# W_out's split weights in slices of h, its row splits one half ahead, and the modulation products spread over the convolutions

## The chip, the cores and the metric

The kernel runs on one core of one Trainium2 chip. The core has TensorE (PE, matrix products; PEld is its weight load), VectorE (DVE), ScalarE (ACT), GpSimd (POOL) and SyncE (SP, here a queue that issues DMAs). The engines run independently, each through its own queue in order, and wait for each other by semaphores. The metric is the device time of one execution in microseconds (us).

## The reference

One layer of an encoder over 1024 rows of 1024 features, all in float32:

```python
mod = c_act @ w_ada + b_ada
sh_m, sc_m, g_m, sh_f, sc_f, g_f = split(mod, 6)
h = rmsnorm(x, norm_mix_w) * (1 + sc_m) + sh_m
z, xbc, dt_raw, q, k, v = split(h @ w_in)
y_ssd = ssd_mixer(z, xbc, dt_raw, ...)      # causal conv width 4, silu, state-space scan, gate, norm
y_att = chunk_attention(q, k, v, rel_bias)  # 8 heads of 64, own chunk and 8 before
x = x + g_m * (concat[y_ssd, y_att] @ w_out)
h = rmsnorm(x, norm_ffn_w) * (1 + sc_f) + sh_f
x = x + g_f * conv_ffn(h, w_up, ffn_conv_w, w_down)
return rmsnorm(x, final_norm_w)
```

## The kernel before

Every large product is made of three TensorE products (`mm3`, lines 56 to 58): each float32 operand is split into a rounded high part and a low rest (`split`, lines 65 and 66: ACT writes the high part, DVE or POOL the rest), and high x high, high x low and low x high are added up. A tile is 128 rows by up to 512 columns. The order of the instructions on each engine is made by a planner, which simulates the program with its own costs and issues what is ready by them; `tc.issue_after(i)` adds the rule that something comes behind instruction i on i's engine.

The stages in order:

1. The norm of x, h = `hth`, `htl` (eight feature blocks by 1024 rows, high and low), and q, k, v of head pairs 0 and 1.
2. `attention(p)` for four pairs of heads, in steps u = 0 to 3 of two row tiles. Pairs 2 and 3 get their q, k, v by products put between the steps of pairs 1 and 2. `attention(3)` has none; there the modulation products are issued.
3. A modulation product is `mod_col`: a load of one 128 x 1024 block of w_ada on SP, and one DVE instruction (line 114) that multiplies it by the activated c and sums along the rows. Of 48 column blocks, 16 are made in stage 1. `MODS` says how many are made in each step of `attention(3)`, from four buffers of the tag qk. The last eight (`G_F`) come in four of the convolutions, two each, from the buffers `wos`.
4. Eight calls of `conv_silu` (B, C and the SSD inputs): a product of h with a block of W_in into one of two PSUM tiles `s`, then ACT (L421), three DVE sums (L423), tanh on ACT (L428) and two DVE products (L429). Each has its weights loaded by `wu_pair` (L129) and split by ACT and POOL.
5. z = h @ W_z in two column halves, `z_tile(1, st)` and `z_tile(0, st)`, st the row tile. Each reads column slice st of `hth` and `htl`. Beside the second half come `row_of` (turns eight columns of the gate into a row broadcast over partitions), `dt_prep` (softplus of dt, decays), the first chunk's `ssd_pre`, and the first W_out weights.
6. The SSD scan, chunk by chunk (`ssd_chunk`), and the output product, row tile by row tile (`wout_tile`), which the planner lays between each other. W_out is cut into eight pieces (dh, j): column half dh, and two of the eight feature blocks. Each piece is loaded, multiplied by the gate row on DVE (L518, the fold) and split (L65, L66). y_a's rows (part 0) and the SSD's (part 1, in `xs`) are split beside the products (`yh`, `yl`). After the tile follow the sum with x (L748) and `norm_row`.
7. The feed-forward part: w_up with the gated convolution, w_down, the final norm.

Before, two W_out pieces (column half 0, y_a) are split into the buffers `wh`, `wl` of the convolution weights; the other six go to tiles `woh`, `wol` of the pool `wop`, which takes the space of `hth` and `htl` and opens when z is done. The staged raw pieces lie in `wos` (three) and `raws` (two).

## Time and profile before

| | |
|---|---|
| median of 3 runs | 1259.03 us (1258.4 to 1260.23) |
| the profiled execution | 1259.93 us, span 1258.2 us |
| mean granted TensorE clock | 0.982 |
| PE busy | 1181.4 us (94%), 5786 products |
| PEld busy | 988.0 us (79%) |
| DVE busy | 954.1 us (76%) |
| ACT busy | 560.3 us (45%) |
| POOL busy | 196.6 us (16%) |
| DMA | 150.86 MB, mean 120 GB/s |

The profile is of one execution. Its slices are 40 equal parts of the span, with the busy share in tenths. A stage table gives the busy time of each engine between two times, then the granted TensorE clock (1.00 is full speed), the share of time that the DMA engines were busy, and GB/s. A row of the waits names who waited for whom, the total, how often, and the longest. Products on TensorE overlap at their ends, so that the duration of one (389 ns) is longer than the step from one to the next.

### The profile page before, as it was taken

The page shows a single profiled execution, that of the slowest core. Times are in us where ns is not written, and L with a number is a line of the kernel's source. Part 1 is how long each engine was busy: PE and PEld are TensorE (multiplying, and loading weights), DVE is VectorE, ACT ScalarE, POOL GpSimd, SP SyncE. Part 2 cuts the span into 40 slices and gives each one's busy share as a digit, 9 for nine tenths or more (in the row PEclk, how much of TensorE's full clock was granted, in tenths as well). Part 3 has the DMA queues.
Part 4 walks back from the last instruction along what each step waited for, and adds up shares of the span by engine and source line. Part 5 has one row for each costly group of instructions (what it writes and reads, how often), then busy time and mean ns, then how long its engine had stood idle before and what let it go on. Part 6 is the DMA issues. An engine that isn't in the chain of part 4 may idle for free.

```text
span 1258.2 us, 15608 instructions
## 1 busy us (share of the span) xinstructions
PE 1181.4 (94%) x5786; PEld 988.0 (79%) x5786; DVE 954.1 (76%) x1452; ACT 560.3 (45%) x917; POOL 196.6 (16%) x174
## 2 busy tenths in 40 slices
PE   5898999979999979999799999999999999999995
PEld 3686788857889968888578888888888888888884
DVE  7836554599576886764999898888898879766976
ACT  4526554653333453434644444533344435433443
POOL 1304563764120032210000000000000000000002
PEclk9999999999999989999999999999999999999998
DMA  9712121336232212221213322223323286834433
GB/s 341 257 25 66 56 61 45 128 124 228 84 99 104 102 34 67 68 67 67 92 42 126 126 95 93 90 101 126 126 78 107 84 300 225 301 107 137 163 122 133
DMA packets 57835, 150.86 MB, mean 120 GB/s; under 512 B 5792, under 2 KB 5920, under 8 KB 56352
## 3 DMA queue, kind: packets, MB, share of 16 engines
q1 hardware_dynamic: 50704, 125.49, 29.3%
q10 hardware_dynamic: 7056, 24.38, 4.8%
q8 instruction: 45, 0.74, 0.2%
q14 instruction: 30, 0.25, 0.1%
HBM read 116.56 MB, written 29.10 MB: 116 GB/s over the span
## 4 chain that ended last, share of the span: by engine, by line
PE 80%; DVE 11%; ACT 3%; issue 2%; DMA 2%; POOL 0%; SPq 0%; DVEq 0%; POOLq 0%; ACTq 0%
PE dn L57 6%; PE dn L56 6%; PE dn L58 5%; PE uY L56 5%; PE uY L58 5%; PE uY L57 5%; PE uZ L58 3%; PE uZ L57 3%; PE uZ L56 3%; PE uX L58 3%; PE uX L57 3%; PE uX L56 3%; PE acc L56 3%; PE acc L57 3%; PE acc L58 3%; PE wops L56 2%
## 5 line engine op out<-in xcount | busy, mean ns | idle before, releaser
L765 POOL TENSOR_TENSOR st<-st,mhalf 128x1 f32<-128x1 f32 x16 | 12.4, 777 | 679.5 <-DVE st L764 679.5
L56 PE MATMUL dn<-w 128*128 128x512 f32 x308 | 111.9, 389 | 0.0
L57 PE MATMUL dn<-w 128*128 128x512 f32 x308 | 111.9, 389 | 0.0
L325 POOL TENSOR_SCALAR p<-p,st 128x640 f32<-128x640 f32 (+4 forms) x64 | 103.0, 1623 | 31.5 <-DVE st L324 26.2
L58 PE MATMUL dn<-w 128*128 128x512 f32 x308 | 103.3, 389 | 0.0
L65 ACT ACTIVATE w<-ya 128x1024 fp32r<-128x1024 f32 (+1 forms) x44 | 41.8, 950 | 98.4 <-PE uY L58 89.5
L56 PEld LDWEIGHTS dn<-w 128*128 128x128 f32 x308 | 57.8, 188 | 12.0
L58 PEld LDWEIGHTS dn<-w 128*128 128x128 f32 x308 | 57.8, 188 | 12.0
L57 PEld LDWEIGHTS dn<-w 128*128 128x128 f32 x308 | 57.8, 188 | 11.9
L65 ACT ACTIVATE w<-xs 128x1024 fp32r<-128x1024 f32 (+1 forms) x44 | 41.8, 951 | 40.5 <-PE uY L58 30.1
L319 DVE CUSTOM_DVE_ANT_0 p<-s,bias 128x640 f32<-128x640 f32 (+4 forms) x64 | 40.6, 650 | 23.5 <-PE tp L351 8.7
L65 ACT ACTIVATE pt<-tp 128x512 fp32r<-128x512 f32 (+2 forms) x72 | 36.4, 522 | 48.4 <-PE tp L351 23.3
L66 DVE TENSOR_TENSOR pt<-tp,pt 128x512 fp32r<-128x512 f32 (+2 forms) x72 | 41.9, 596 | 20.4 <-ACT pt L65 13.3
L322 ACT ACTIVATE p<-p,st 128x640 f32<-128x640 f32 (+4 forms) x64 | 44.1, 690 | 21.1 <-DVE st L319 20.2
L66 DVE TENSOR_TENSOR w<-ya,w 128x1024 fp32r<-128x1024 f32 (+1 forms) x44 | 47.8, 1087 | 5.1 <-ACT w L65 5.1
L56 PE MATMUL s<-hth,wh 128*128 128x512 f32 x128 | 51.6, 403 | 0.2 <-DVE bt L423 0.2
L907 DVE SCALAR_TENSOR_TENSOR a<-cv,pkt,a 128x1023 f32<-128x1023 f32 (+1 forms) x40 | 51.1, 1277 | 0.1
L57 PE MATMUL s<-htl,wh 128*128 128x512 f32 x128 | 51.0, 398 | 0.0
L58 PE MATMUL s<-hth,wl 128*128 128x512 f32 x128 | 50.8, 396 | 0.0
L907 DVE SCALAR_TENSOR_TENSOR a<-cg,pkt,a 128x1023 f32<-128x1023 f32 (+1 forms) x40 | 49.5, 1278 | 0.0
L66 POOL TENSOR_TENSOR wl<-raws,wh 128x1024 fp32r<-128x1024 f32 x14 | 33.9, 2422 | 89.0 <-ACT wh L65 89.0
L66 DVE TENSOR_TENSOR w<-xs,w 128x1024 fp32r<-128x1024 f32 (+1 forms) x44 | 47.7, 1085 | 0.0
(410 smaller groups left out, 3592.1 us busy)
## 6 DMA issues: line engine op xcount, KB each, us to landing
qk<-in_w_ada_dram SPq DMA_DIRECT2D x24, 512.0 KB, 4.7
gz<-a ACTq DMA_DIRECT2D x10, 1024.0 KB, 5.3
adat<-in_w_ada_dram SPq DMA_DIRECT2D x16, 512.0 KB, 5.7
ya<-in_w_up_dram SPq DMA_DIRECT2D x10, 768.0 KB, 4.0
xs<-in_w_up_dram SPq DMA_DIRECT2D x10, 768.0 KB, 4.0
raws<-in_w_ft_dram SPq DMA_DIRECT2D x14, 512.0 KB, 3.5
gy<-a ACTq DMA_DIRECT2D x10, 512.0 KB, 2.6
qk<-in_x_dram SPq DMA_DIRECT2D x8, 512.0 KB, 6.3
```

The costliest lines, as they stand in the source:

```text
L56: T.matmul(ps, lh, rh, start=start, stop=False, skip_group_check=more)
L57: T.matmul(ps, lh, rl, start=False, stop=False, skip_group_check=more)
L58: T.matmul(ps, ll, rh, start=False, stop=stop, skip_group_check=more)
L65: i = A.activation(hi, src, AF.Copy) if ehi is A else ehi.tensor_copy(hi, src)
L66: return i, elo.tensor_tensor(lo, src, f32(hi), ALU.subtract)
L319: V.tensor_tensor_reduce(out=dst, in0=src, in1=bsl, scale=-1.0, scalar=3e38, op0=ALU.add, op1=ALU.min, accum_out=nm)
L322: A.activation(pv_, pv_, AF.Exp, scale=-1.0, bias=nm, accum_out=rs)
L325: G.tensor_scalar(pv_, pv_, rr, None, op0=ALU.mult)
L765: G.tensor_tensor(r, ms, mhalf[:, 0:1], ALU.pow)
L907: V.scalar_tensor_tensor(a[:, j:S], c[:, 0:S - j], w[2 - j], a[:, j:S], op0=ALU.mult, op1=ALU.add)
```

## The change

- Modulation: `MODS` goes from (0, 4, 4, 16) to (0, 2, 2, 10), with the gate of the mixer first; the other 18 products, G_F's eight among them, are made after each of the eight convolutions (`CMODS`, 2 or 3 each) from the three `wos` buffers. `affn` and `bffn` are computed after the z stage.
- W_out: every piece is split into a slice of `hth` and `htl` of 128 columns (slot j of the order `WORDER`), over all eight feature blocks. Slot j is read by z row tile j, so it is free once that tile is done in both halves. Raw pieces lie in a ring of three `wos` and two `raws` buffers. The gate row and the first three loads and folds move to the first z half; the splits of these three come behind `dt_prep`'s own split (`pin`), the other five folds and splits behind the last ACT and DVE instructions of the first `ssd_pre`. `dt_prep` moves from z row tile 2 to 0 of the second half, `ssd_pre` from 4 to 3, the second gate row from 1 to 3. The pool of h is closed only after the feed-forward sums.
- `wout_tile`: the split rows of y lie in one tile (two buffers, in the convolution weights' space), and are made one half-tile ahead of their products; x comes as one 128 x 1024 load in place of two of 128 x 512.

```diff
@@ -23,10 +23,10 @@
 FFN = 2816
 NF = FFN // P
 EPS = 1e-6
-WZB, ROWST, ROWST2, DTST, WOST = 4, 0, 1, 2, 3
+WZB = 4
 PB = (2, 2, 1, 3)
-FOLD = (1, 1, 1, 1)
-MODS = (0, 4, 4, 16)
+MODS = (0, 2, 2, 10)
+CMODS = (2, 2, 2, 2, 2, 2, 3, 3)
 PRST = 4
 GP, GPL = {0: (0,1), 2: (2,)}, ()
 XL = (3, 4, 5, 6)
@@ -370,7 +370,7 @@
                         tl.rearrange("p (a b) -> p a b", a=2), ALU.add)
 
     last_v, early = [], {}
-    mtq, todo = [], [(m + kt) for kt in range(KT) for m in (G_M, SC_F, SH_F)]
+    mtq, todo = [], [m + kt for m in (G_M, SC_F, SH_F, G_F) for kt in range(KT)]
 
     def attention(p, extra=()):
         extra = dict(extra)
@@ -468,11 +468,20 @@
     na = bcp.tile([P, 16], F32, name="na")[:, 0:8]
     wos = bcp.tile([P, 3, D], F32, name="wos")
     es_t = ExitStack()
+    wosc, stc_, pin = [0], [0], []
+
+    def stage():
+        i, stc_[0] = stc_[0] % 5, stc_[0] + 1
+        return wos[:, i, :] if i < 3 else raws[:, i - 3, :]
+
+    def conv_mods(n, at):
+        for _ in range(CMODS[n]):
+            wosc[0] += 1
+            mod_col(todo.pop(0), wos[:, wosc[0] % 3, :], at)
+
     for g in range(2):
-        conv_silu(4 + g, bt_[g], th512)
-        conv_silu(6 + g, ct_[g], th512)
-    mod_scale(affn, SC_F, NFFN, 0, KT)
-    mod_shift(bffn, SH_F, 0, KT)
+        conv_mods(2 * g, conv_silu(4 + g, bt_[g], th512))
+        conv_mods(2 * g + 1, conv_silu(6 + g, ct_[g], th512))
     sgt_ = th512()[:, 0:P]
     G.memset(ones, 1.0)
     G.affine_select(out=tle, in_=ones, compare_op=ALU.is_ge, fill=0.0, base=0,
@@ -483,9 +492,7 @@
     sgt = f32(sgtr)
     for ft in range(4):
         xt = bcp.tile([P, S], F32, tag="rm", bufs=2, name="xst")
-        at = conv_silu(ft, xt, th512)
-        for i in range(2):
-            mod_col(G_F + 2 * ft + i, wos[:, i, :], at)
+        conv_mods(4 + ft, conv_silu(ft, xt, th512))
         for hh in range(2):
             tps = tp_tile()
             for j in range(4):
@@ -493,33 +500,25 @@
                             ident)
             A.activation(xs[:, 4 * hh:4 * hh + 4, ft * P:(ft + 1) * P],
                          tps.rearrange("p (a b) -> p a b", a=4), AF.Copy)
-    wop_ = []
-    wosc = [0]
     halves = [slice(0, 512), slice(512, 1024)]
     order = [4, 5, 6, 7, 0, 1, 2, 3]
-
-    def wout_weights(dh, js):
-        ws = []
-        for j in js:
-            if dh == 0 and j < 2:
-                wh = wu.tile([P, 1024], F32R, tag="wh", name="wh")
-                wl = wu.tile([P, 1024], F32R, tag="wl", name="wl")
-            else:
-                wh = wop_[0].tile([P, 1024], F32R, tag=f"woh{dh}{j}", name="woh")
-                wl = wop_[0].tile([P, 1024], F32R, tag=f"wol{dh}{j}", name="wol")
-            if (dh, j // 2) != (0, 0) and wosc[0] < 3:
-                t = wos[:, wosc[0], :]
-                wosc[0] += 1
-            else:
-                t = raw_tile()
-            for b in range(2):
-                nc.sync.dma_start(t[:, b * 512:(b + 1) * 512], w_out[order[2 * j + b], :, halves[dh]])
-            tv = t.rearrange("p (a b) -> p a b", a=2)
-            (V if FOLD[j] else G).tensor_tensor(
-                tv, tv, rowb[:, halves[dh]].unsqueeze(1).to_broadcast([P, 2, 512]), ALU.mult)
-            split(wh, wl, t, A, V)
-            ws += [(wh[:, 0:512], wl[:, 0:512]), (wh[:, 512:1024], wl[:, 512:1024])]
-        return ws
+    ws = [[], []]
+
+    def wout_load(dh, j):
+        t = stage()
+        for b in range(2):
+            nc.sync.dma_start(t[:, b * 512:(b + 1) * 512], w_out[order[2 * j + b], :, halves[dh]])
+        return t
+
+    def wout_fold(dh, t):
+        tv = t.rearrange("p (a b) -> p a b", a=2)
+        V.tensor_tensor(tv, tv, rowb[:, halves[dh]].unsqueeze(1).to_broadcast([P, 2, 512]), ALU.mult)
+
+    def wout_split(dh, t, slot):
+        c = slice(slot * P, slot * P + P)
+        with tc.issue_after(pin[0]), tc.issue_after(pin[1]):
+            split(hth[:, :, c], htl[:, :, c], t.rearrange("p (a b) -> p a b", b=P), A, V)
+        ws[dh] += [(hth[:, k:k + 4, c], htl[:, k:k + 4, c]) for k in (0, 4)]
 
     def rm512():
         return bcp.tile([P, S], F32, tag="rm", bufs=2, name="gt")[:, 0:512]
@@ -575,7 +574,7 @@
         V.scalar_tensor_tensor(sm["adt"].rearrange("p (c h) -> p c h", c=8),
                                sm["dt"].rearrange("p (c h) -> p c h", c=8), -1.0,
                                na.unsqueeze(1).to_broadcast([P, 8, 8]), op0=ALU.mult, op1=ALU.mult)
-        split(adh, adl, sm["adt"], A, V)
+        pin[:] = [i.ins for i in split(adh, adl, sm["adt"], A, V)]
         dps = tp_tile()
         for i, m in enumerate((tle, sgt, ones)):
             T.matmul(dps[:, 64 * i:64 * i + 64], m, sm["adt"], start=True, stop=True)
@@ -614,39 +613,47 @@
             for i in range(2):
                 T.matmul(sg, sgtr, rm[:, i].rearrange("p h l -> p (h l)"), start=i == 0, stop=i == 1)
             m = th512().rearrange("p (h l) -> p h l", h=4)
-            A.activation(m, sg.rearrange("p (h l) -> p h l", h=4), AF.Exp)
-            V.tensor_tensor(m, m, cb[:, g:g + 1, :].to_broadcast([P, 4, P]), ALU.mult)
+            pin1 = A.activation(m, sg.rearrange("p (h l) -> p h l", h=4), AF.Exp)
+            pin2 = V.tensor_tensor(m, m, cb[:, g:g + 1, :].to_broadcast([P, 4, P]), ALU.mult)
             ms_.append(m)
+        pin[:] = [pin1.ins, pin2.ins]
         return xdt, xdd, cb, ms_
 
     wz = wz_weights(1)
+    gcol = const.tile([P, 16], F32, name="gcol")
+    gbias = [pkt[:, B_ADA + o:B_ADA + o + 8] for o in (G_M, G_F)]
+    V.tensor_tensor(gcol[:, 0:8], modc[:, G_M:G_M + 8], gbias[0], ALU.add)
+    WORDER = [(0, 0), (0, 1), (1, 0), (1, 1), (0, 2), (0, 3), (1, 2), (1, 3)]
+    wt = []
     for st in range(NT):
         z_tile(1, st, wz)
+        if st == 0:
+            row_of(gcol[:, 0:8], rowb, ps1, "tp", 2, ones, rm512)
+            wt += [wout_load(*w) for w in WORDER[0:3]]
+        if st in (3, 4, 5):
+            wout_fold(WORDER[st - 3][0], wt[st - 3])
     wz = wz_weights(0)
-    gcol = const.tile([P, 16], F32, name="gcol")
-    gbias = [pkt[:, B_ADA + o:B_ADA + o + 8] for o in (G_M, G_F)]
-    V.tensor_tensor(gcol[:, 0:8], modc[:, G_M:G_M + 8], pkt[:, B_ADA + G_M:B_ADA + G_M + 8], ALU.add)
     for st in range(NT):
         z_tile(0, st, wz)
-        if st == ROWST:
-            row_of(gcol[:, 0:8], rowb, ps1, "tp", 2, ones, rm512)
-        if st == DTST:
+        if st == 0:
             dt_prep()
-        if st == ROWST2:
+        if st == 3:
+            for j in range(3):
+                wout_split(WORDER[j][0], wt[j], j)
+            pre0 = ssd_pre(0, tp_tile, tp_tile)
             V.tensor_tensor(gcol[:, 8:16], modc[:, G_F:G_F + 8], gbias[1], ALU.add)
             row_of(gcol[:, 8:16], rowa, ps1, "tp", 2, ones, rm512)
-        if st == PRST:
-            pre0 = ssd_pre(0, tp_tile, tp_tile)
-        if st == WOST:
-            ws0 = wout_weights(0, (0, 1))
+    for j in range(3, NT):
+        wt.append(wout_load(*WORDER[j]))
+        with tc.issue_after(pin[1]):
+            wout_fold(WORDER[j][0], wt[j])
+        wout_split(WORDER[j][0], wt[j], j)
     es_t.close()
     es_p1.close()
-    es_ht.close()
 
 
     es_w = ExitStack()
     wop = es_w.enter_context(tc.tile_pool(name="wop", bufs=1, side="left", reuse_waits="tile"))
-    wop_.append(wop)
     es_p2b = ExitStack()
     ps2b = es_p2b.enter_context(tc.tile_pool(name="ps2b", bufs=1, space=PSUM, side="left",
                                              reuse_waits="tile"))
@@ -726,35 +733,38 @@
             for j, g in enumerate(names):
                 gd[g, m] = t[:, :, j, :]
 
-    ws = [ws0, []]
-    ws[1] += wout_weights(1, (0, 1))
-    ws[0] += wout_weights(0, (2, 3))
-    ws[1] += wout_weights(1, (2, 3))
+    mod_scale(affn, SC_F, NFFN, 0, KT)
+    mod_shift(bffn, SH_F, 0, KT)
+    xr_, yq, dg = {}, {}, {}
+
+    def wout_rhs(st, part):
+        if st < NT:
+            y = yq[st, part] = wu.tile([P, 2, 4, P], F32R, tag="wh", name="yhl")
+            split(y[:, 0], y[:, 1], x1[part][:, st, :].rearrange("p (a b) -> p a b", a=4), A, V)
+
     def wout_tile(st):
-        xr = [wop.tile([P, 512], F32, tag="xr", bufs=2, name="xr") for _ in range(2)]
-        for dh in range(2):
-            nc.sync.dma_start(xr[dh], x[st * P:(st + 1) * P, halves[dh]])
+        xr = xr_[st] = wu.tile([P, 2, 512], F32, tag="wl", name="xr")
+        nc.sync.dma_start(xr.rearrange("p a b -> p (a b)"), x[st * P:(st + 1) * P, :])
         ps = [ps2b.tile([P, 512], F32, tag="wo", bufs=PB[0], name="wops") for _ in range(2)]
+        if st == 0:
+            wout_rhs(0, 0)
         for part in range(2):
-            yh = wop.tile([P, 4, P], F32R, tag="yh", bufs=3, name="yh")
-            yl = wop.tile([P, 4, P], F32R, tag="yl", bufs=3, name="yl")
-            split(yh, yl, x1[part][:, st, :].rearrange("p (a b) -> p a b", a=4), A, V)
+            y = yq.pop((st, part))
+            wout_rhs(st + part, 1 - part)
             for dh in range(2):
                 for k in range(4):
                     w = ws[dh][4 * part + k]
-                    mm3(ps[dh], yh[:, k, :], yl[:, k, :], w[0], w[1], part == 0 and k == 0,
-                        part == 1 and k == 3)
+                    mm3(ps[dh].rearrange("p (a b) -> p a b", a=4), y[:, 0, k, :], y[:, 1, k, :],
+                        w[0], w[1], part == 0 and k == 0, part == 1 and k == 3)
         for dh in range(2):
-            V.tensor_tensor(x1[dh][:, st, :], ps[dh], xr[dh], ALU.add)
+            V.tensor_tensor(x1[dh][:, st, :], ps[dh], xr[:, dh, :], ALU.add)
             nc.scalar.dma_start(x1d[st * P:(st + 1) * P, halves[dh]], x1[dh][:, st, :])
 
-    dg = {}
-
     def norm_row(st):
-        junk = wop.tile([P, 512], F32, tag="xr", bufs=2, name="junk")
+        junk = xr_.pop(st)
         m = [stat(), stat()]
         for dh in range(2):
-            A.activation(junk, x1[dh][:, st, :], AF.Square, scale=1.0 / 32.0, accum_out=m[dh])
+            A.activation(junk[:, dh, :], x1[dh][:, st, :], AF.Square, scale=1.0 / 32.0, accum_out=m[dh])
         r = rstd2(m)
         dg[st] = wop.tile([P, P], F32, tag="dg", bufs=8, name="dg")
         V.tensor_scalar(dg[st], ident, r, None, op0=ALU.mult)
@@ -964,6 +974,7 @@
     h_raw((7,))
     sums(slice(384, 512))
     es_w.close()
+    es_ht.close()
     es_l.close()
     fp = ctx.enter_context(tc.tile_pool(name="fp", bufs=1, side="left", reuse_waits="tile"))
     c_tile("v")
```

## The prediction

> **What bounds the kernel now.** I read the 40 slices (31.5 us each) first, then busy time by stage, then TensorE's waits and the queues around the worst of them.
>
> ```profile
> PE   5898999979999979999799999999999999999995
> DVE  7836554599576886764999898888898879766976
> 262.00:284.00 22.00, 13.59 (x79) 12.24 (x78) 21.48 (x54) 11.60 (x27) 17.19 (x8) 0.87 0.54 189
> 284.00:316.00 32.00, 29.74 (x155) 25.07 (x155) 30.14 (x51) 10.94 (x20) 14.84 (x6) 0.98 0.64 216
> 316.00:391.00 75.00, 75.00 (x360) 62.87 (x360) 46.11 (x59) 26.71 (x42) 10.72 (x7) 0.98 0.31 106
> 391.00:414.00 23.00, 23.00 (x192) 22.76 (x191) 13.24 (x27) 6.83 (x15) 0.00 (x0) 1.00 0.14 48
> 414.00:442.30 28.30, 28.30 (x218) 26.44 (x217) 24.81 (x48) 14.51 (x37) 2.05 (x2) 1.00 0.32 112
> 442.30:463.50 21.20, 14.75 (x62) 10.81 (x60) 16.82 (x19) 13.28 (x28) 9.24 (x7) 0.76 0.15 51
> 463.50:570.00 106.50, 103.75 (x531) 87.61 (x532) 72.85 (x115) 37.49 (x97) 25.30 (x33) 1.00 0.18 60
> 600.00:640.00 40.00, 30.97 (x139) 24.23 (x138) 39.56 (x55) 22.62 (x32) 0.00 (x0) 0.96 0.18 64
> ```
>
> The stage rows give length, then busy time of PE, PEld, DVE, ACT, POOL, then granted clock and DMA. PE is the bound nearly everywhere. It dips to 7 tenths in three slices after the start (numbers 9, 15 and 20). The first (the last head pair's attention, 262 to 316) and the third (600 to 640) are stages in which DVE has no free time. In the second, where z ends and W_out begins (442.3 to 463.5), PE stands still for 21.20 - 14.75 = 6.45 us. The change touches the first two and leaves the third. What stands still costs twice, by the clock:
>
> ```profile
> 266.00:268.00 2.00, 0.73 (x6) 0.49 (x4) 2.00 (x5) 1.37 (x3) 2.00 (x1) 1.00 0.12 25
> 268.00:270.00 2.00, 0.00 (x0) 0.00 (x0) 2.00 (x3) 0.00 (x0) 1.18 (x1) 1.00 0.90 295
> 272.00:274.00 2.00, 2.00 (x9) 1.96 (x9) 2.00 (x7) 1.98 (x5) 1.91 (x2) 0.50 0.91 354
> 282.00:284.00 2.00, 2.00 (x12) 2.00 (x11) 1.71 (x6) 1.23 (x3) 2.00 (x2) 0.50 0.86 326
> 316.00:318.00 2.00, 2.00 (x6) 1.52 (x6) 1.94 (x4) 1.07 (x3) 0.00 (x0) 0.50 0.49 184
> 452.00:454.00 2.00, 1.22 (x2) 0.50 (x2) 2.00 (x2) 1.79 (x7) 1.80 (x2) 0.50 0.01 5
> ```
>
> After each standstill comes a stretch at half clock. A 22 us stage at 0.87 lost 0.13 x 22 = 2.9 us of clock, 32 us at 0.98 lost 0.6, the next 75 us at 0.98 lost 1.5: 5.0 us around the attention. The stretch at 0.76 lost 0.24 x 21.2 = 5.1, of which about 70% (14.75 of 21.20) fell on work: 3.6.
>
> **Term A, modulation products out of the attention.** 24 products are issued there now (4, 4, 16 by step), 14 after (2, 2, 10). They sit ahead of the attention's own DVE work in a queue that runs in order. (Group rows: line, engine, operation, output and inputs, count, then busy us and mean ns, then idle time before and who ended it. Timeline rows: start, duration, instruction, idle before in brackets.)
>
> ```profile
> L114 DVE CUSTOM_DVE_ANT_0 qk<-qk,rows 128x1024 f32<-128x1024 f32 x24 | 30.8, 1318 | 1.3 <-DMA qk<-in_w_ada_dram 1.1
> 266.62 1.22 DVE L114 CUSTOM_DVE_ANT_0 qk<-qk,rows 128x1024 f32<-128x1024 f32 x1
> 271.04 0.43 PE L362 MATMUL pv<-pt,v 128*128 128x256 f32 x1 [4.31 <-DVE ya L368]
> 280.07 0.33 PE L351 MATMUL tp<-ident,p 128*128 128x128 f32 x1 [3.66 <-DVE pt L66]
> 314.39 0.33 PE L363 MATMUL pv<-pt,v 128*128 128x128 f32 x1 [2.00 <-DVE pt L66]
> 311.40 2.59 DVE L423 SCALAR_TENSOR_TENSOR bt<-s,pkt,bt 128x1023 f32<-128x1023 f32 x2
> ```
>
> Taking 2 products out of a burst of 4 frees 2 x 1.318 = 2.6 us: the wait of 4.31 falls to 1.7, that of 3.66 to 1.0, together 5.2 us. The 2.00 wait comes from convolution sums (L423) that start late, at 311.4, behind the last burst; 6 x 1.318 = 7.9 us fewer products ahead of them take it away whole. The three half-clock stretches (5.0) go if what is left of the waits is too short to trip the clock. The rows say it is: 1.27 us idle in 266 to 268 was followed by 268 to 270 still at 1.00. Upper end: 5.2 + 2.0 + 5.0 = 12.2. Lower end: only the two burst gains, with 1.2 given back to reordered queues, 4. DVE's own work in the two stages, 51.6 us of 54, falls by 10 x 1.318 = 13.2 to 38.4; PE's 43.3 less the clock's 3.5 is 39.8. Both fit in 42, so the upper end isn't excluded. I take 9, three quarters, since the attention keeps chains that nothing fills.
>
> The Trainium skill, "TensorE: Matmul & The Clock Gate", Part 1 (The HAM clock gate), says that the clock falls to half after at least one idle window of about 3.4 us, and that this window runs freely. The trace agrees on half clock, but not on a whole window: the 2.00 us wait before 314.39 was enough for 0.50 at 316. By that rule the third half-clock stretch would not be there to win, a third of 5.0 less and 1244.7 in all; by the row it counts.
>
> **Term B, W_out's weights.** Eight pieces are each loaded, folded with the gate (L518, DVE) and split (L65 ACT, L66 DVE). Before, six of the splits have to wait for the pool that opens when all of h is released at 442.3, and they all land at once:
>
> ```profile
> L66 DVE TENSOR_TENSOR wol<-wos,woh 128x1024 fp32r<-128x1024 f32 x3 | 4.9, 1655 | 0.5 <-ACT woh L65 0.5
> L66 DVE TENSOR_TENSOR wol<-raws,woh 128x1024 fp32r<-128x1024 f32 x3 | 3.6, 1216 | 1.1 <-ACT woh L65 1.1
> L518 DVE TENSOR_TENSOR raws<-raws,rows 128x1024 f32<-128x1024 f32 x5 | 6.1, 1223 | 0.6 <-DMA raws<-in_w_out_dram 0.5
> PE wops L56 <- ACT yh L65: 6.1, 7, 2.6
> 454.74 0.80 PE L58 MATMUL wops<-wh,yl 128*128 128x512 f32 x1 [0.96 <-DVE yl L66]
> 461.41 0.60 PE L709 MATMUL xps<-ident,yy 128*128 128x128 f32 x4
> 462.05 0.69 DVE L710 TENSOR_TENSOR xs<-xps,pkt 128x512 f32<-128x512 f32 x1 [2.09 <-PE xps L709]
> 463.46 0.50 PE L56 MATMUL wops<-woh,yh 128*128 128x512 f32 x1 [0.78 <-ACT yh L65]
> ```
>
> DVE carries 4.9 + 3.6 + 1.2 = 9.7 us of W_out here. The row halves of y_a (yh, yl) queue behind them, the first product block cannot run until 454.74, and the SSD chunk's transposes, behind it on PE, come at 461.41. After the change piece j goes into columns j of h, free once z row tile j is done. Three are folded during the first z half (391 to 414, where DVE is busy 13.24 of 23, so 3 x 1.22 and the gate row moved with them are covered), split behind the dt chain; the other five are pinned behind the SSD prelude on ACT and DVE. What is queued behind those pins is only W_out; who waits is the wops products. Piece 7 needs the last z tile, so I count three splits (3.7 us) left after z. DVE in the stretch: 16.82 - 9.7 + 3.7 = 10.8. PE's work at full clock is 14.75 - 3.6 = 11.1. Both chained need some 13, against 21.2: a gain of 8. Ends: 6.45 + 3.6 = 10.0 if all idle and clock loss go, and 0 if ACT and DVE are issued the late splits first again. I take 7.5. In the z stage itself DVE loses two folds and the gate row and gains one to three splits, so 24.81 of 28.3 stays about the same; PE is covered there by four z accumulators.
>
> W_out's moving operand becomes four blocks of 128 columns, a row of h apart. No row shows TensorE reading so; the nearest are ACT writing such blocks and writing plain ones:
>
> ```profile
> L494 ACT ACTIVATE xs<-tp 128x512 f32<-128x512 f32 x8 | 4.4, 595 | 7.4 <-PE tp L492 7.2
> L125 ACT ACTIVATE rows<-rowps 128x512 f32<-128x512 f32 x4 | 2.4, 593 | 3.9 <-PE rowps L124 3.9
> L56 PE MATMUL wops<-woh,yh 128*128 128x512 f32 x96 | 38.5, 401 | 3.5 <-ACT yh L65 3.5
> L56 PE MATMUL dn<-w 128*128 128x512 f32 x308 | 111.9, 389 | 0.0
> ```
>
> 595 against 593: blocks cost nothing, and I take 0. For an upper end, two plain groups of the same shape already differ by 12 ns; times 384 products that is 4.6 us. A gain is excluded: as many columns are read.
>
> **Term C, row splits one half ahead.** From 463.5 to 570 PE idles 106.5 - 103.75 = 2.75 us, all waits of wops for yh. Issued a half earlier some of them go, but the half that comes from xs still waits for the SSD chain. Between 0 and 2.75 I take 1.5. Two buffers instead of three, and x loaded as one tile into the freed conv-weight buffers, cost nothing: the tile before last is done. SP issues 8 x loads in place of 16; W_out's 16 stay 16, the first six behind the last product that uses their buffers. POOL's queue is not passed by anything.
>
> **Term D, products in the convolutions.** Ten more there, each 1.22 us:
>
> ```profile
> L114 DVE CUSTOM_DVE_ANT_0 wos<-wos,rows 128x1024 f32<-128x1024 f32 x8 | 9.5, 1221 | 0.0
> L423 DVE SCALAR_TENSOR_TENSOR xst<-s,pkt,xst 128x1023 f32<-128x1023 f32 (+2 forms) x12 | 15.4, 1282 | 8.6 <-ACT xst L421 8.3
> L429 DVE SCALAR_TENSOR_TENSOR xst<-th,xst 128x512 f32<-128x512 f32 x8 | 5.2, 686 | 0.8 <-ACT th L428 0.8
> wos<-in_w_ada_dram SPq DMA_DIRECT2D x8, 512.0 KB, 4.0
> 1064.60 0.91 PE dn L56 x4
> 339.42 0.80 SPq L112 DMA_DIRECT2D wos<-in_w_ada_dram  x2
> ```
>
> 316 to 391 has DVE busy 46.11 of 75, so 12.2 us are covered as work. But every product now needs one of three wos buffers, which open only near the end of the attention (first load at 339.42), takes a load on SP (4.0 us to land), and SP serves the convolutions' weight loads behind it. I charge 2, between 0 and 5. Moved mod_scale and mod_shift, three operations on 128x8, go behind the z stage; the pool that stays open longer delays only buffers needed after 600.
>
> **Sum.** 9 + 7.5 + 1.5 - 2 = 16.0. The profiled run took 1259.93 (span 1258.2), 0.90 above the median of 1259.03; 1259.93 - 16.0 = 1243.9, by the median 1243.0.
>
> **The rivals.**
> *The W_out start stays full.* Pinned pieces come late, and B and C give 0 and 1: 9 + 1 - 2 = 8, 1251. For it: five of eight pieces stand behind the prelude, which itself waits for z's dt columns. Against: dt and prelude lose seven folds ahead of them.
> *The clock still falls.* Waits of 1.7 and 1.0 are left; if both still trip it, two of the three stretches stay: 5.0 x 2 / 3 = 3.4, 1246.4. Against: the 1.27 idle that left the clock at 1.00. For it, the Trainium skill's "TensorE: Matmul & The Clock Gate" (Part 1) has the window run freely, so that a wait can fall either way.
> *It does almost nothing.* Issue order is planned anew; A gives 4, B and C nothing, D takes 4: 1259. For it: DVE is full in both stages. Against: it loses 13 us in the first.
> *Slower: the buffers starve the convolutions.* A convolution holds PE for 48 products of 0.91 / 4 us, 10.9, and DVE 3 x 1.282 + 2 x 0.686 + 2 x 1.221 = 7.7; it decides once DVE waits over 3.2 us per convolution for loads. Two landings waited out in a row (8.0) cost 4.8 each; over five convolutions, 24: 1267. Against: 3 buffers turn in 4.0 + 1.2 + issue, about 6 us, so 18 products take 36 of the 52 us from 339.42 to 391.
>
> **How the numbers follow.** Forecast 0.50, full W_out start 0.16, clock 0.14, almost nothing 0.11, slower 0.09. The range leaves out the slower case and half of "almost nothing" above, and below a gain past 12.2 + 10.0 + 2.75 = 25: 1234 to 1258; the likeliest case alone, between gains of 10 and 23, spans 1236 to 1249. A change under 0.2% (2.5 us) can't be told here from none. Faster: 0.50 + 0.16 + 0.14 and 0.02 of the fourth, 0.82; same, the rest of the fourth, 0.09; slower 0.09.
>
> **What would show it.** A: waits on DVE in the attention below 2 us and no 0.50 after them. B: wops products start within 6 us of z's end, and at most three W_out splits lie behind it. C: fewer waits on yh. D: PE at 75 of 75 through the convolutions. Wrong if PE waits for L423 or weight loads there, if wops products grow past 401 ns, or if the yh splits still queue behind W_out's.

## The result, and the profile after

The changed kernel takes 1250.91 us (median of 4 runs, 1248.69 to 1251.51) against 1259.24 on the same chip: a ratio of 0.993, 95% interval 0.9913 to 0.9948. In a second comparison it took 1250.68 against 1259.1, ratio 0.9933 (0.9921 to 0.9944). So 8.3 us are gained where 16.0 were forecast. The profiled execution took 1251.51, its span is 1249.8. The time lies in the range that was stated (1234 to 1258), but above the likeliest case (1236 to 1249).

The 40 slices of the page after, and six of the stages (clock times are those of before; the work in them has moved earlier by up to 10 us):

```profile
PE   5898999989999989999899999999999999999995
```

```profile
262.00:284.00 22.00, 17.26 (x105) 14.18 (x105) 21.12 (x54) 14.78 (x35) 19.89 (x11) 1.00 0.28 96
284.00:316.00 32.00, 32.00 (x171) 27.26 (x171) 27.78 (x41) 11.20 (x19) 12.52 (x5) 1.00 0.39 133
316.00:391.00 75.00, 73.22 (x382) 62.11 (x381) 61.38 (x79) 26.74 (x42) 13.12 (x7) 1.00 0.51 176
...
442.30:463.50 21.20, 19.66 (x90) 15.96 (x91) 16.01 (x24) 10.44 (x29) 9.12 (x10) 0.92 0.00 1
463.50:570.00 106.50, 103.51 (x537) 87.49 (x536) 70.27 (x113) 37.38 (x97) 24.04 (x33) 1.00 0.18 65
600.00:640.00 40.00, 31.91 (x123) 24.74 (x122) 36.34 (x49) 17.18 (x20) 0.00 (x0) 0.91 0.19 66
```

All three attention rows now stand at a clock of 1.00, and 284 to 316 is full. The convolutions lost their 75 of 75 (73.22). The last row is at 0.91, where before it was at 0.96. TensorE's waits from 255 to 480, with one row from the whole run behind the dots (who waits for whom, total, times, longest):

```profile
PE wops L56 <- DVE zs L551: 4.6, 1, 4.6
PE tp L351 <- DVE pt L66: 2.0, 1, 2.0
PE s L56 <- DVE ct L423: 1.7, 1, 1.7
PE pv L362 <- DVE ya L368: 1.6, 1, 1.6
...
PE wops L56 <- ACT yhl L65: 3.0, 5, 0.6
```

The attention's waits of 4.31 and 3.66 are 1.6 and 2.0 now, and the third one is gone. Two waits are new: 1.7 us for a convolution's sum, and 4.6 us, the longest, of the first W_out product for a gate result of z. The timeline shows why (start, duration, instruction; "x3" is three in a row):

```profile
429.29 2.35 DVE L515 TENSOR_TENSOR raws<-raws,rows 128x1024 f32<-128x1024 f32 x2
431.56 3.48 DVE L515 TENSOR_TENSOR wos<-wos,rows 128x1024 f32<-128x1024 f32 x3
...
435.61 0.28 PE L58 MATMUL s<-wzh,htl 128*128 128x260 f32 x1
...
436.51 2.35 DVE L66 TENSOR_TENSOR htl<-raws,hth 128x1024 fp32r<-128x1024 f32 x2
438.78 3.48 DVE L66 TENSOR_TENSOR htl<-wos,hth 128x1024 fp32r<-128x1024 f32 x3
442.19 0.41 DVE L551 SCALAR_TENSOR_TENSOR zs<-zt,s 128x260 f32<-128x260 f32 x1
443.59 0.64 PE L56 MATMUL wops<-hth,yhl 128*128 128x512 f32 x1 [4.59 <-DVE zs L551]
453.07 0.50 PE L56 MATMUL wops<-hth,yhl 128*128 128x512 f32 x1
```

z's last product ends at 435.9. VectorE then makes the five splits that are pinned behind the prelude (5.8 us) and only afterwards reads z's last two accumulators. W_out's first product waits for that reading (4.59 us): its accumulators take the PSUM space of z's. At 453.07 the second half of W_out's tile 0 begins, which was at 463.46.

Where the time came from, by the same instruction in both traces. The rows of before, then of after, that aren't shown yet. The first is a transpose shortly ahead of the first changed work; up to it TensorE makes the same products in the same order in every version below:

```profile
246.16 0.33 PE L351 MATMUL tp<-ident,p 128*128 128x128 f32 x1 [0.79 <-DVE v L66]
339.11 0.27 PE L363 MATMUL pv<-pt,v 128*128 128x128 f32 x1
389.26 0.48 PE L58 MATMUL s<-hth,wl 128*128 128x512 f32 x1
601.40 0.50 PE L56 MATMUL uX<-b11h,w 128*128 128x512 f32 x1 [0.70 <-ACT w L65]
```

```profile
248.62 0.33 PE L351 MATMUL tp<-ident,p 128*128 128x128 f32 x1 [0.79 <-DVE v L66]
330.16 0.28 PE L363 MATMUL pv<-pt,v 128*128 128x128 f32 x1
381.96 0.40 PE L58 MATMUL s<-hth,wl 128*128 128x512 f32 x1
591.14 0.48 PE L56 MATMUL uX<-b11h,w 128*128 128x512 f32 x1
```

| point | before | after | earlier by | this stretch | forecast |
|---|---|---|---|---|---|
| this transpose starts | 246.16 | 248.62 | -2.46 | +2.46 | 0 |
| attention's last product ends | 339.39 | 330.44 | 8.95 | -11.41 | A -9 |
| convolutions' last product ends | 389.73 | 382.36 | 7.37 | +1.58 | D +2 |
| second half of W_out's tile 0 starts | 463.46 | 453.07 | 10.39 | -3.02 | B -7.5 |
| first feed-forward product starts | 601.40 | 591.14 | 10.26 | +0.13 | C -1.5 |
| end of the span | 1258.19 | 1249.79 | 8.40 | +1.86 | 0 |

The first row is a loss in a part that the change doesn't touch. The clock shows it, 0.98 in place of 1.00 (before, then after):

```profile
72.00:240.00 168.00, 157.55 (x872) 132.84 (x871) 85.74 (x230) 85.96 (x193) 76.74 (x63) 1.00 0.19 52
```

```profile
72.00:240.00 168.00, 158.42 (x861) 133.49 (x860) 85.69 (x230) 85.36 (x191) 76.91 (x63) 0.98 0.19 52
```

In the fourteen profiles of this case the transpose starts between 245.19 and 248.95 us. That is as much as most of the differences between the versions below, so the larger of these are also given from the transpose on.

### The profile page after: what moved, and what is told of

Read it like the earlier page. It is cut to its first block, busy times and chain, and to the rows that moved or that the text cites. A ratio compares the mean times of both kernels' runs of the same rounds, so it can differ in the third digit from the quotient of the medians.

```text
span 1249.8 us, 15597 instructions
## 1 busy us (share of the span) xinstructions
PE 1180.4 (94%) x5786; PEld 986.6 (79%) x5786; DVE 959.6 (77%) x1452; ACT 559.7 (45%) x917; POOL 202.8 (16%) x174
## 4 chain that ended last, share of the span: by engine, by line
PE 79%; DVE 12%; ACT 3%; DMA 2%; issue 2%; POOL 1%; SPq 0%; DVEq 0%; POOLq 0%; ACTq 0%
PE dn L56 6%; PE dn L57 6%; PE dn L58 6%; PE uY L56 5%; PE uY L57 5%; PE uY L58 5%; PE uZ L57 3%; PE uZ L58 3%; PE uZ L56 3%; PE uX L57 3%; PE uX L58 3%; PE uX L56 3%; PE acc L56 3%; PE acc L57 3%; PE acc L58 3%; PE wops L56 2%
## 5 line engine op out<-in xcount | busy, mean ns | idle before, releaser
L56 PE MATMUL wops<-hth,yhl 128*128 128x512 f32 x128 | 51.6, 403 | 7.7 <-DVE zs L551 4.6
L66 DVE TENSOR_TENSOR pt<-tp,pt 128x512 fp32r<-128x512 f32 (+2 forms) x72 | 41.7, 595 | 18.0 <-ACT pt L65 10.8
L57 PE MATMUL wops<-htl,yhl 128*128 128x512 f32 x128 | 51.0, 398 | 0.0
L58 PE MATMUL wops<-hth,yhl 128*128 128x512 f32 x128 | 50.4, 404 | 0.0
```

The costliest lines, as they stand in the source:

```text
L56: T.matmul(ps, lh, rh, start=start, stop=False, skip_group_check=more)
L57: T.matmul(ps, lh, rl, start=False, stop=False, skip_group_check=more)
L58: T.matmul(ps, ll, rh, start=False, stop=stop, skip_group_check=more)
L66: return i, elo.tensor_tensor(lo, src, f32(hi), ALU.subtract)
```

## Experiments

Theory after the result: A and D give what was forecast or more. B is short because VectorE's order at the end of z puts five splits ahead of what TensorE needs first. C is nothing. The first and the last stretch are lost to the clock. The rivals: the modulation products carry the whole gain; VectorE is simply full there, so that no order helps; the half-ahead splits take part of B. Each ratio below is to the kernel before on the same chip, with its 95% interval. A measure used throughout is the stretch from z's last product to the second half of W_out's tile 0: 21.1 us before, 17.2 after.

**The modulation part alone**, on the kernel before:

```diff
-MODS = (0, 4, 4, 16)
+MODS = (0, 2, 2, 10)
+CMODS = (2, 2, 2, 2, 2, 2, 3, 3)
...
+        conv_mods(2 * g, conv_silu(4 + g, bt_[g], th512))
```

> The kernel before with the modulation part alone (products 2, 2, 10 in the attention, 18 in the convolutions). Theory 1, the gains lie in two separate places and add: z starts 6.5 us earlier than before, as in the changed kernel, and nothing is won behind it, 1252.5 (1251 to 1254). Theory 2, all of the gain is the modulation's: 1251, and the stretch between z and W_out shrinks too because DVE arrives less late. Theory 3, the W_out part brought it: 1258 to 1260.

1255.39 us, 0.9963 (0.9951 to 0.9976). In its profile z ends 6.58 us earlier, the first feed-forward product starts 6.47 earlier, and the span ends 4.69 earlier. The stretch after z is as before (21.1). The first theory had z right and the time too short (1251 to 1254): 1.8 us are lost again in the feed-forward part.

**The W_out part alone**, on the changed kernel:

```diff
-MODS = (0, 2, 2, 10)
-CMODS = (2, 2, 2, 2, 2, 2, 3, 3)
+MODS = (0, 4, 4, 16)
+CMODS = (0, 0, 0, 0, 2, 2, 2, 2)
```

> The changed kernel with the modulation products where they were (4, 4, 16 in the attention, 8 in four convolutions): the W_out part alone. Theory 1: the last z product comes when it does before, the first row tile's second half starts 3.5 to 4 us earlier, 1255.5 (1254 to 1257.5). Theory 2: 1258 to 1260. Theory 3: 1251.

1258.16 us, 0.999 (0.9979 to 1.0001): no difference that can be told. Its waits:

```profile
PE wops L56 <- DVE zs L551: 4.6, 1, 4.6
PE pv L362 <- DVE ya L368: 4.3, 1, 4.3
PE tp L351 <- DVE pt L66: 3.8, 1, 3.8
PE pv L363 <- DVE pt L66: 2.4, 2, 2.0
```

The attention's old waits are back beside W_out's new one. The stretch after z is 18.1, and the first feed-forward product starts 2.90 earlier; then 2.47 of that are given back before the end. The first theory (3.5 to 4 us, 1254 to 1257.5) had too much; the time fits the second, which gives the whole gain to the modulation, but the stretch after z speaks against that one. Up to the feed-forward part the two halves nearly add up (6.47 + 2.90 = 9.4 against 10.26). Counted from the transpose (at 247.49 and 246.15) it is 7.8 + 2.9 = 10.7 against 12.7; the 2 us between them are lost where the modulation part alone has a half-clock stretch in the convolutions (316 to 391 at 0.98). At the end the halves don't add up (4.69 + 0.43 against 8.40), because each kernel loses about 2 us in the feed-forward's first 40 us, and the sum counts this twice.

**Row splits at their own half**, on the changed kernel:

```diff
-        if st == 0:
-            wout_rhs(0, 0)
         for part in range(2):
+            wout_rhs(st, part)
             y = yq.pop((st, part))
-            wout_rhs(st + part, 1 - part)
```

> The changed kernel with the row splits made at their own half instead of one ahead. Theory 1, the half ahead is worth nothing since five waits of about 0.55 us on the splits are still there: 1250 to 1252. Rival: it keeps the first split off the splits of W_out's pieces and so carries part of the gain at the start: 1253 to 1255, with a wait of 2 us or more for the first yhl.

1249.65 us, 0.9921 (0.9906 to 0.9935): no slower. The row of W_out's waits for yhl is the same to the tenth (3.0, 5, 0.6). The half ahead is worth nothing: with it and without it there are five waits of 0.6.

**z's gate first**: the splits of pieces 4 to 7 are pinned behind z's last gate product on VectorE.

```diff
+            with tc.issue_after(zl[0]) if j > 3 else ExitStack():
-        wout_split(WORDER[j][0], wt[j], j)
+                wout_split(WORDER[j][0], wt[j], j)
```

> The changed kernel with the splits of W_out pieces 4 to 7 put behind z's last evacuation on DVE, nothing else. Theory 1, the 4.6 us in which PE waits for zs are the queue on DVE (five splits ahead of two evacuations): the wait falls under 1.5 us, no half clock follows, and the run takes 1246 to 1248. Rival, the pieces themselves are late: the wait goes over to htl or hth and the run stays at 1250 to 1252.

1249.95 us, 0.9921 (0.9905 to 0.9937). The order does what it should, and nothing is won:

```profile
PE xps L717 <- DVE yy L714: 3.9, 1, 3.9
...
PE wops L56 <- DVE zs L551: 1.5, 1, 1.5
```

W_out's first product starts 4.6 us after z's last one in place of 7.7, but the wait moves on to the SSD chunk, whose normalised y (`yy`) now comes behind the splits. The stretch after z is 17.8, no better than 17.2.

**The late pieces behind chunk 0 too**: piece 4 behind z, pieces 5 to 7 behind y*zs of the first chunk.

```diff
+        yz = V.tensor_tensor(y, y, zs[:, c, 0:512], ALU.mult)
+        if c == 0:
+            for j in range(5, NT):
+                with tc.issue_after(yz.ins), tc.issue_after(za[0]):
+                    wout_split(WORDER[j][0], wt[j], j)
```

> On the changed kernel: the splits of pieces 5 to 7 go behind chunk 0's product y*zs on VectorE and behind the last gate's tanh on ScalarE; piece 4's stays behind the last gate product. Theory (VectorE's order at the start of W_out is what cost the gain; the two chains that TensorE needs first are the gate's evacuation and the first SSD chunk): both waits shrink, the one on zs (4.6 us after the change) below 2 and the one on yy (3.9 us with pieces 4 to 7 behind z) below 2 as well, and the second half of W_out's tile 0 starts 5 to 8 us earlier relative to z's end than before, in place of 3.9: 1246 to 1248 us. Rival (VectorE is simply full there, order only moves the wait): the wait turns up at wops for the last pieces' weights (htl or hth) with 3 us or more, and the time is 1250.

1247.99 us, 0.9909 (0.9896 to 0.9922). The wait on zs is gone and the stretch after z is 15.6, 5.5 less than before in place of 3.9: the first theory's times, just. But 2.6 of the 2.7 us between its span (1246.3) and that of the changed kernel's second profile (1249.0) are there at the transpose already (245.26 against 247.86). What is won after z is nearly all lost elsewhere, most of it in the convolutions, where the wait for ct is 2.0 and a half-clock stretch follows (0.57 from 344 to 348). And the theory's second wait didn't go: 3.4 us on yy stay. GpSimd's row of the timeline shows what holds yy:

```profile
443.28 1.20 POOL L96 TENSOR_SCALAR st<-st 128x1 f32<-128x1 f32 x1
444.56 1.39 POOL L97 TENSOR_TENSOR st<-st,mhalf 128x1 f32<-128x1 f32 x1
```

The chunk's scale is two operations on 128x1, and beside the splits on VectorE they take 1.20 and 1.39 us.

**One burst**: the 14 products that stay in the attention go into its last step.

```diff
-MODS = (0, 2, 2, 10)
+MODS = (0, 0, 0, 14)
```

> On the changed kernel: the 14 products that stay in the last attention are all issued in its last step (0, 0, 0, 14 by step) in place of 2, 2, 10. Theory (each burst stands ahead of the attention's own softmax work in VectorE's queue): the waits of 2.0 (transposes) and 1.6 us (pv) go, and attention's last pv comes 2 to 3.5 us earlier; the convolution sums L423 come 4 products, 5 us, later behind the longer last burst, and the wait of 1.7 us on ct grows by less than that. 1248 to 1250 us. Rival (the burst's length at the last step decides, as it did before with 16): a wait of 2 us or more returns there with a half-clock stretch behind it, and the time is 1251 to 1253.

1244.95 us, 0.9889 (0.9876 to 0.9901), better than expected. Its longest wait from 255 to 480 behind that on zs:

```profile
PE s L56 <- DVE bt L423: 1.3, 1, 1.3
```

Both attention waits are gone, and the one on L423 fell instead of growing. z ends at 431.1, 4.8 us earlier than in the changed kernel; 2.4 of these are there at the transpose already (246.23), where nothing was changed. The other 2.4 are not where the theory had them: the attention's last product comes at 331.1, 0.6 us later and not 2 to 3.5 earlier, and the gain shows in the convolutions and z. The wait of 4.6 on zs is untouched.

**Convolutions: the products late**.

```diff
-CMODS = (2, 2, 2, 2, 2, 2, 3, 3)
+CMODS = (1, 1, 1, 1, 3, 3, 4, 4)
```

> On the changed kernel: the 18 products of the convolutions come as 1, 1, 1, 1, 3, 3, 4, 4 in place of 2, 2, 2, 2, 2, 2, 3, 3. Theory (the products that follow each convolution delay the next one's sums L423 on VectorE): the wait of 1.7 us on ct L423 goes, nothing new comes in the later convolutions, and the time falls by 1 to 1.7 us: 1249.3 to 1250. Rival (loads of the wos pieces, not the products, hold the convolutions): the wait stays or moves to the last convolutions, no difference, 1250.9.

1245.85 us (1243.55 to 1250.68), 0.9898 (0.988 to 0.9915). The wait on ct L423 is gone, as expected, and the one on pt is 0.7 in place of 2.0. These make 3.0 us; z ends 4.25 earlier, and 2.3 of that are there at the transpose (246.34), where nothing was changed. The 2.0 that are left are near the 1 to 1.7 expected; the median gained more, over runs that lie 7 us apart.

**The changed kernel again**, for its clock.

> The changed kernel itself, for the comparison on this chip: 1250 to 1252 us. Its profile is wanted for the half-clock stretches. If a stretch outside the changed stages (at 105.9 for 6.8 us in the first profile) is a matter of where the clock's window happens to fall, it is not at the same place with the same length here, and the time between the last wops product and the end differs by 1 to 2 us between the two profiles. If the change itself caused it, it is there again.

1250.68 us. The half-clock stretch at 105.9 is there again, at 104.8, and as long (6.8 us). By the expectation the change then causes it, but the other profiles speak against that: between 72 and 240 the clock is 1.00 in seven of the fourteen, six of them with the whole change or a part of it, and 0.98 in the other seven. Two versions below are the same program up to there, the burst with the late pieces behind chunk 0 and the one with them behind the normalised y; the first has 1.00, the second 0.98. One run of the changed kernel, that of 1248.69 us, has a mean clock of 0.988, where the other eight have 0.982 to 0.985. What decides is open.

**Both moves of the products.**

> The changed kernel with both moves of the modulation products at once: 0, 0, 0, 14 in the last attention and 1, 1, 1, 1, 3, 3, 4, 4 in the convolutions. Alone they gave 1245.0 and 1245.9 against 1250.7, with z's end 4.1 and 3.6 us earlier in their profiles. Theory 1 (they remove different waits: the first those of 2.0 and 1.6 in the attention, the second that of 1.7 on the convolution sums): together z ends 5 to 7 us earlier than in the changed kernel and the time is 1242 to 1244. Theory 2 (both end in the same place: once the convolutions' start is smooth, TensorE is the bound up to z and what is left is only its work): no more than the better one alone, 1244.5 to 1246.

1246.44 us, 0.9897 (0.9874 to 0.992). z ends at 430.0, only 1.0 us before the burst alone, and the time is no better. Against the changed kernel that is 5.8 us, as the first theory had it; from the transpose (245.70) to z's end it is 2.9, against 2.4 and 2.0 for each move alone. So the two don't add up, and the second theory holds, though the time is just above its 1246: after either move little waiting is left ahead of z.

**The burst, and the late pieces behind chunk 0.**

> The one burst of 14 together with the order at W_out's start in which pieces 5 to 7 are split behind chunk 0's y*zs. In that order alone the chunk's normalisation took 4.7 us on GpSimd beside the splits (its two operations on 128x1 took 1.20 and 1.39 us where they take 0.24 and 0.57 otherwise, behind a state update of 2.02). Theory (order at W_out's start gains little and is independent of the attention): the wait of 4.6 on zs goes, one of 3 to 4 on yy comes, and the time is 2 to 3 us below the burst alone: 1242 to 1243.5. Rival (with one burst the z stage is already so full of VectorE work that order makes no difference): 1244.5 to 1246.

1242.96 us, 0.9876 (0.9851 to 0.99). It has the lowest median of all versions, and it beats both kernels: its ratio to the kernel before is 0.9876, that of the changed kernel 0.993. Against the burst alone the intervals overlap; from the transpose (245.54) to the end its profile is 3.2 us shorter. The wait on zs is gone, 3.4 on yy have come, as expected, and the stretch after z is 14.9. In its stage row the W_out start has lost its half-clock stretch:

```profile
442.30:463.50 21.20, 20.20 (x106) 16.57 (x106) 16.12 (x27) 9.06 (x24) 5.86 (x7) 1.00 0.15 49
```

**The late pieces behind the normalised y**, so that VectorE makes no splits while GpSimd works on the scale:

```diff
-        yz = V.tensor_tensor(y, y, zs[:, c, 0:512], ALU.mult)
+        yz = V.tensor_scalar(y, y, r, None, op0=ALU.mult)
```

> As the burst with pieces 5 to 7 behind y*zs, but behind the normalised y of chunk 0 instead, so that VectorE does no splits while GpSimd works on the chunk's scale. Theory (the two engines slow each other there): GpSimd's two operations on 128x1 fall back to 0.24 and 0.57 us, the wait on yy falls from 3.4 to under 2, and TensorE next waits for the last pieces' weights (htl) by 0 to 3 us, as 5.2 us of splits now start some 2 us later: 1240.5 to 1243. Rival (no contention; the state update ahead of it on GpSimd alone holds the chunk): the two operations stay at 1.2 and 1.4, and the late splits cost 2 to 4 us: 1245 to 1247.

1248.16 us, 0.9903 (0.988 to 0.9926): 5.2 us more than behind y*zs. Between the two profiles it is 5.5, and 3.4 of that are there at the transpose (248.95 against 245.54), so they are not the order's. The stretch after z is 16.5, 1.6 more than 14.9. The timeline and the waits:

```profile
442.57 0.23 POOL L96 TENSOR_SCALAR st<-st 128x1 f32<-128x1 f32 x1
442.89 0.57 POOL L97 TENSOR_TENSOR st<-st,mhalf 128x1 f32<-128x1 f32 x1
...
PE wops L56 <- ACT yhl L65: 4.9, 2, 4.3
...
PE xps L722 <- DVE yy L715: 1.0, 1, 1.0
```

The theory's mechanism is right (1.20 and 1.39 fall to 0.23 and 0.57, the wait on yy to 1.0), its sum is wrong: the splits now stand ahead of `xs` and its row split, and TensorE waits 4.3 for that.

**Two and two**: piece 5 behind y*zs, 6 and 7 behind the row split of tile 0's second half.

```diff
+            if (st, part) == (0, 1):
+                for j in (6, 7):
+                    with tc.issue_after(i[0].ins), tc.issue_after(i[1].ins):
+                        wout_split(WORDER[j][0], wt[j], j)
```

> As the burst with the late pieces behind chunk 0's y*zs, but only piece 5 there; pieces 6 and 7, which the second column half of tile 0 reads, go behind the row splits of tile 0's second half (yhl from xs). Theory (on VectorE the chain of chunk 0, its xs and its yhl must come first, and each piece just before its product block): VectorE has 1.2 to 1.8 us of splits beside GpSimd's scale in place of 5.2, the wait on yy falls from 3.4 to about 1, nothing waits over 1 us for htl, and the second half of tile 0 starts 1 to 2 us earlier relative to z's end: 1241 to 1242.5. Rival (the second half needs as much VectorE work before it as there is time, whatever its order): a wait of 2 us or more on yhl or htl takes the place of that on yy, 1243 to 1246.

1291.27 us, 1.0257 (1.0241 to 1.0273). Up to tile 0's second half it does what was expected (stretch 13.5, wait on yy 2.0). Then W_out stands still:

```profile
539.81 2.35 DVE L66 TENSOR_TENSOR htl<-wos,hth 128x1024 fp32r<-128x1024 f32 x2
...
463.50:532.00 68.50, 38.68 (x152) 31.09 (x150) 36.96 (x53) 16.08 (x44) 15.90 (x19) 0.70 0.00 1
```

Pieces 6 and 7 are split at 531 (high part) and 540 (low part), some 90 us late. In the program they now stand behind all eight SSD chunks, and the planner put them there; a pin says what must come before, not by when. The chunks ran without W_out's products between them, with TensorE busy 38.68 of 68.50 at a clock of 0.70. It doesn't test the order that was meant.

## Why the prediction was right or wrong

**A, the mechanism right, the size too small: 11.4 for 9.** That the attention's last product comes 8.95 us earlier, just the 9 of the forecast, is luck: 2.46 us had been lost ahead of the attention, at the lower clock, which is in no term of the sum. From the transpose on A is 11.4, near its upper end of 12.2, and 11.2 to 11.7 in the six other profiles with the same 14 products in the same steps. The waits left are 1.6 where 1.7 was forecast and 2.0 where it was 1.0, and no half-clock stretch follows them:

```profile
276.00:278.00 2.00, 0.55 (x3) 0.31 (x3) 2.00 (x7) 0.25 (x1) 2.00 (x1) 1.00 0.58 174
278.00:280.00 2.00, 1.98 (x15) 1.85 (x16) 1.94 (x6) 1.07 (x3) 2.00 (x2) 1.00 0.82 285
```

The bound on the waits (below 2 us) was met only just. A wait of 1.97 left the clock at 1.00 here, where one of 2.00 was followed by 0.50 before. The 1.62 ahead of pv left it at 1.00 too, but in the kernel with the convolutions' products late, and in the modulation part alone (0.66 from 270 to 275), nearly the same wait (1.62 and 1.61) was followed by half clock:

```profile
268.03 0.39 PE L362 MATMUL pv<-pt,v 128*128 128x256 f32 x1 [1.62 <-DVE ya L368]
...
270.00:272.00 2.00, 1.91 (x10) 1.80 (x9) 2.00 (x10) 1.63 (x5) 2.00 (x2) 0.59 0.48 190
```

So the rival "the clock still falls" did not happen, but the step that set it aside doesn't exclude it: the row with 1.27 us idle is the head of the wait of 4.31 us (266.73 to 271.04), and that wait did end at half clock. Waits of this size fell either way, in two of seven profiles to half clock; what decided is not shown. The Trainium skill, "TensorE: Matmul & The Clock Gate", Part 1 (The HAM clock gate), with its freely running window of about 3.4 us, agrees: equal waits can fall either way. These rows don't bear it out that a whole idle window is needed: all five waits were shorter than one, and three were followed by half clock.

**B, the size was wrong: 3.0 of 7.5.** The failed step is "I count three splits (3.7 us) left after z". Five were left, as the five folds ran until 435.0, and the sum "both chained need some 13" took no account of order: it compared busy times. Its own sign, a W_out product within 6 us of z's end, failed too (7.7). VectorE needed 12.95 us for what it did from 435.9 to 453.1, of 17.2; with the two more splits the prediction's 10.8 would have been 13.2, so the busy time was right. What stood in the way was which piece came first:

```profile
435.90:453.10 17.20, 12.49 (x61) 9.95 (x60) 12.95 (x18) 8.76 (x21) 12.88 (x7) 0.90 0.06 24
```

W_out's products waited for z's own evacuation. The prediction named who waits for the pins ("only W_out") and missed that `zs`, which is not pinned, can be issued behind them, and that W_out's accumulators stand on z's PSUM tile. Two orders that remove or shorten the wait show the same bound from two sides: with the splits behind z alone the SSD chunk waits (3.9); with them behind y*zs the stretch is 15.6 and 14.9. The forecast 13.6 was reached only by the start of the last kernel (13.5), which lost far more behind it. Of the 4.5 us missed, order gave back 1.6 to 2.3; the rest is not settled.

The strided moving operand costs nothing, as taken: W_out's groups run at 403, 398 and 404 ns, against 401, 394 and 402 for the same groups before; where both are undisturbed, from 490 to 560, at 397, 391 and 401 against 399, 392 and 404.

```profile
L56 PE MATMUL wops<-hth,yhl 128*128 128x512 f32 x128 | 51.6, 403 | 7.7 <-DVE zs L551 4.6
...
L114 DVE CUSTOM_DVE_ANT_0 wos<-wos,rows 128x1024 f32<-128x1024 f32 x18 | 25.8, 1466 | 2.7 <-DMA wos<-in_w_ada_dram 2.7
```

**C, wrong: nothing for 1.5.** From 463.5 to 570 TensorE is busy 103.51 of 106.50, before 103.75. The step "issued a half earlier some of them go" fails: the five waits are all for the half that comes from xs. ACT has stood idle for over 4 us until VectorE writes xs (one of the five):

```profile
470.12 0.63 ACT L65 ACTIVATE yhl<-xs 128x512 fp32r<-128x512 f32 x1 [4.24 <-DVE xs L717]
470.80 0.50 PE L56 MATMUL wops<-hth,yhl 128*128 128x512 f32 x1 [0.55 <-ACT yhl L65]
```

Before, ACT waited for xs in the same way (4.24 us at 480.10). The prediction named this ("still waits for the SSD chain") and gave the term 1.5 all the same. Undoing the half ahead left the five waits unchanged.

**D, right in size (1.6 for 2), not in place.** The charge was for loads that land late. VectorE did wait 2.7 us for them in all (the second row above), but TensorE waited for L423 (1.7), that is for the products that stand between a convolution's sums, each 1.47 us in the mean where 1.22 was taken. Putting them later took the wait away, while VectorE waited as long for its first load there (3.06 us). By the prediction's own sign D's mechanism was wrong. The operations for `affn` didn't go behind the z stage either: in the program they stand there, but in the trace one of them, on 128x8, comes at 336.51 among these products and takes 2.24 us.

**Not in the sum: 2.5 us ahead of the attention and 1.9 at the end.** The first is told above. The prediction left 600 to 640 alone. Between the same two points there (601.4 to 649.6 before, 591.1 to 641.2 after) TensorE waited as long, 9.0 us and 9.1, but the clock went from 0.96 to 0.93:

```profile
614.00:618.00 4.00, 4.00 (x12) 3.14 (x11) 4.00 (x5) 2.65 (x4) 0.00 (x0) 0.57 0.00 0
...
628.00:632.00 4.00, 4.00 (x12) 3.10 (x12) 3.53 (x6) 0.88 (x1) 0.00 (x0) 0.57 0.56 218
```

Before, this stage had one half-clock stretch of 3.4 us, now it has two. In the traces of all experiments it has two, or one twice as long, those included that have only one half of the change. Where a stretch falls is shown; that it would fall elsewhere if the stage came at another time is only argued.

The time that came out, 1250.91, is the one that the rival "the W_out start stays full" gave (1251), by half of its mechanism: the late pins held W_out, but B was 3.0 and not 0, A was 2.4 more than its 9, and 4.3 were lost at a lower clock in parts of which the sum says nothing.

## What to carry to other kernels

Removing work from a queue that runs in order gains where the work stood ahead of what the bound engine needs next; the waits that end there, and the clock behind them, were a good estimate. For a stage in which two engines are both nearly full, a sum of busy times gives only a floor: write down the order in which the bound engine needs the other's results, include the evacuations that free its accumulators, and pin moved work behind those too. A pin gives an earliest place and no latest one. Before a few microseconds between two versions are put down to an edit, compare the time at which the first changed work starts in both: here it differed by up to 3.8 us.

## What the runs showed of the hardware

GpSimd and VectorE slow each other. Two 128x512 products on GpSimd took 8.32 us beside VectorE's five splits in the changed kernel, and 3.77 where one and a part of a second ran beside them (the kernel with the burst and the late pieces behind chunk 0). In that kernel three splits took 5.18 us beside GpSimd's work on the chunk, where three take 3.48 in the changed kernel:

```profile
435.85 8.32 POOL L687 TENSOR_TENSOR yy<-xs,pkt 128x512 f32<-128x512 f32 x2 [9.76 <-PE s L57]
```

```profile
429.60 3.77 POOL L689 TENSOR_TENSOR yy<-xs,pkt 128x512 f32<-128x512 f32 x2 [9.77 <-PE s L57]
...
436.19 5.18 DVE L66 TENSOR_TENSOR htl<-wos,hth 128x1024 fp32r<-128x1024 f32 x3
```

The 4.55 us between the two GpSimd rows are near the time of the three to four splits more (3.48 for three in a row). The Trainium skill, "Trainium Architecture — The Big Picture", What this means for kernel authors, says that the two share a pair of ports under "an exclusive lock (not a bandwidth split)"; these numbers agree with it, but don't exclude a division of bandwidth.

Half-clock stretches of 3.4 or 6.8 us can appear in a stage that wasn't touched, and be missing there in the next version: the rows from 72 to 240 above have a clock of 1.00 and 0.98 for the same products in the same order. In the seven profiles with 1.00 there the transpose starts between 245.19 and 246.16 us, in the seven with 0.98 between 246.23 and 248.95. Differences of this size are as large as the smaller terms of a sum like this one.
